# Sample-token products over 128 rows instead of 32, whole-identity transposes, and two vector transposes merged

## The chip, the core and the metric

The kernel runs on one core of a Trainium2 chip. The core has five engines with a queue each: PE (TensorE: matrix products and transposes; the profile shows its weight loads apart, as PEld), DVE (VectorE), ACT (ScalarE), POOL (GpSimd) and SP (SyncE, which here only issues DMAs). They run side by side and meet at semaphores. The metric is the time of one execution on the device in microseconds (us), as a median of several runs. Smaller is better.

## The reference: what is computed

One encoder layer for two requests at once: a prompt of 1024 tokens and 32 sample tokens that go on from a cache. Model width is 1024, everything is float32. Cut to what matters:

```python
h  = rms_norm(x, g_pre_mix);  z = h @ w_in          # q, k, v | q, f, i, og | two gates
# A: windowed attention, 16 query heads, 2 key/value heads of width 64, a sink per head
s  = q @ k.T * 64**-0.5 + bias                      # sample: 128 cached + 32 new keys
m  = max(s.max(-1), sink);  p = exp(s - m)
ya = (p / (p.sum(-1) + exp(sink - m))) @ v
# B: gated linear recurrence, 8 heads, key and value width 128, blocks of 64 (sample: 32)
o  = (q * exp(b)) @ state
a  = (q * exp(b - b_mid)) @ (k * exp(b_mid - b)).T
o  = o + where(causal, a, 0) @ v
state = exp(b_last) * state + (k * exp(b_last - b)).T @ v
yb = rms_norm(o, g_hgrn_out) * silu(og)
x  = x + rms_norm((sig(ga) * (ya @ w_br_a) + sig(gb) * (yb @ w_br_b)) @ w_out)
# conv feed-forward, then a per-layer input behind a gate
x  = x + rms_norm((gelu(conv3(a)) * u) @ w_down);  x = x + (pe @ w_ple) * sig(x @ w_ple_gate)
```

## The kernel before

Tokens lie along the free axis of most tiles, features along the 128 partitions. The 1056 tokens (1024 prompt, then 32 sample) are cut into the groups `GR` of 384, 384 and 288 columns. `token_tiles(g)` cuts a group into tiles of 128; the third tile of group 2 is the sample with its 32 tokens.

Large products run in three passes over a high and a low part of both operands (`product`, lines 200 to 202, in the first stages; lines 1006 to 1009 in the recurrence). One pass is one PE matmul with a stationary operand of 128 rows by 128 columns, which PEld loads, and 288 or 384 moving columns. A matmul of two plain float32 operands is issued as two PE instructions; a float32 transpose (a matmul against the identity `ident`) as one. In a row of the profile, "32*128 32x32" means: 32 rows contracted, 128 stationary columns, and 32 moving columns.

The stages that the change touches, in order of time:

- **Start, up to about 59 us.** Rows of `x` are loaded, normed and transposed. `turn_(g, k, b)` (line 584) transposes block k of the up to three row tiles of group g; for group 2 the third transpose has 32 rows. `h_part` (ACT line 226, DVE line 227) splits the result into `La` and `Lb`, which the products read, and `x_store` (DVE line 593) writes the scaled block away. `norm_rows` (line 301) spreads a column of factors over all partitions; its third product for group 2 has 32 rows (it is called later with tiles of 88 and 96 rows too). `vectors` (line 617) transposes four small tiles of gains and caches: 8, 41, 88 and 44 rows. `step` and `pinned` fix the order of work on the engines named; the rest is ordered by the framework's planner, from estimated times.
- **Attention, about 57 to 375 us.** A stream of products (`stream`), with the attention of one head pair i beside it. For each i from 0 to 7 and each block j from 0 to 8, `scores(i, j)` makes the probabilities in a tile `sc` (lines 451 to 467; POOL writes the sink at line 455), `turn(i, j)` transposes them (line 478) and splits them into `ph` and `pl` (ACT 223, DVE 224), and `values(i, js)` multiplies them with `Vs` (lines 500 and 501). Block j = 8 is the sample: 32 query rows, and keys in two tiles, 128 cached ones and 32 new ones (tile 9 of `Vs`).
- **Recurrence, about 375 to 870 us.** 8 heads; 22 pieces of products per head, and beside them the recurrence of the head before. `k_turn` and `v_turn` (lines 1174, 1102) transpose the decayed keys and the values of a group into `kk` and `vk`; `tile_in(h, j)` computes the state update (line 1192) and the scores (1200, for the sample 1196), masks them into `am`, and updates the state; `tile_out(h, j)` computes the output (lines 1232 and 1234); `group_out(h, g)` transposes it back (line 1255). j = 8 is the sample: 32 rows at lines 1192, 1232 and 1255, and 32 stationary columns at 1196, 1232 and 1234.

Each of these PE instructions has its operands cut to the tile's own number of rows `m_`:

```python
E.transpose(b[:, n * P:n * P + rows], t[:rows, k * P:(k + 1) * P], ident[:rows, :rows])   # turn_
E.matmul(oc, lhs, ph[:kn, a, :2 * m_], start=a == 0, stop=False)          # values, lhs = Vs[:kn, ...]
E.matmul(s[:, 256:384], kk[:m_, i, :], vk[:m_, i, :], start=True, stop=True)              # tile_in
E.matmul(b[:m_, 0:P], am[:m_, :m_], vk[:m_, i, :], start=True, stop=st is None)           # tile_out
E.transpose(t[:, c:c + m_], vk[:m_, i, :], ident[:m_, :m_])                               # group_out
```

Of the kernel before, what the change touches and what calls it, by code (L numbers as in the profile page):

```python
# [10 lines left out]
F32 = mybir.dt.float32  # L11
# [6 lines left out]
P = 128  # L18
# [41 lines left out]
def layer_kernel(  # L60
# [251 lines left out]
    with right("ap") as ap:  # L312
# [130 lines left out]
        def scores(i, j):  # L443
            m_, k0, nk, b0, tl = span(j)
            e_ = b0 + nk
            g, c = (2, SO) if j == 8 else (j // 3, (j % 3) * P)
            kv, bias = i // 4, biases[i]
            s = s_bank()
            for h, q in enumerate(qs[i, g]):
                o = s[:, h * 256 + b0:h * 256 + e_]  # L450
                E.matmul(o, q[:, c:c + P], K1[kv][:, k0:k0 + nk], start=True, stop=False)
                E.matmul(o, q[:, c:c + P], K2[kv][:, k0:k0 + nk], start=False, stop=True)
            sc = aq.tile([P, 2, 260], F32, tag="sc", name=nm("sc"), bufs=5)
            st = aq.tile([P, 2, 2], F32, tag="st", name=nm("st"), bufs=4)
# [13 lines left out]
            probs[i, j] = sc  # L468

        def turn(i, j):  # L470
            m_, k0, nk, b0, tl = span(j)
            sc = probs[i, j]
            ph = aq.tile([P, 2, 2 * P], F32R, tag="ph", name=nm("ph"), bufs=4)
            pl = aq.tile([P, 2, 2 * P], F32R, tag="pl", name=nm("pl"), bufs=4)
            t = tr_bank()
            for a, (_, kc, kn) in enumerate(tl):
                for h in range(2):
                    E.transpose(t[:kn, a * 256 + h * m_:a * 256 + (h + 1) * m_],  # L478
                                sc[:m_, h, kc:kc + kn], ident[:m_, :m_])
            if m_ == P:  # L480
                sl = [(P, slice(0, 256 * len(tl)))]
            else:
                sl = [(kn, slice(a * 256, a * 256 + 2 * m_)) for a, (_, _, kn) in enumerate(tl)]
            fh, fl = ph[:].rearrange("p a b -> p (a b)"), pl[:].rearrange("p a b -> p (a b)")
            for kn, z in sl:
                split(fh[:kn, z], fl[:kn, z], t[:kn, z])
            probs[i, j] = (ph, pl)

        def values(i, js):
# [4 lines left out]
            for x, j in enumerate(js):  # L494
                ph, pl = probs.pop((i, j))
                tl = span(j)[4]
                oc = o[:, x * 256:x * 256 + 2 * m_]
                for a, (vt_, _, kn) in enumerate(tl):
                    lhs = Vs[:kn, vt_, kv].rearrange("p a b -> p (a b)")
                    E.matmul(oc, lhs, ph[:kn, a, :2 * m_], start=a == 0, stop=False)  # L500
                    E.matmul(oc, lhs, pl[:kn, a, :2 * m_], start=False, stop=a == len(tl) - 1)
            nx = len(js)
# [36 lines left out]
        with tc.tile_pool(name="np", bufs=1, side="right", reuse_waits="tile") as np_:  # L539
            def load_tile(xt, g, n):  # L540
                t = np_.tile([P, D], F32, tag="x", name=nm("x"), bufs=8)
                xt.append((t, load_x(t, g, n, x_prompt, x_sample)))

# [37 lines left out]
            def turn_(g, k, b):  # L581
                hb[g, k] = b
                for n, (t, rows) in enumerate(xt[g]):
                    E.transpose(b[:, n * P:n * P + rows], t[:rows, k * P:(k + 1) * P],
                                ident[:rows, :rows])

# [9 lines left out]
            def vector_rows():  # L596

                g0 = np_.tile([8, P], F32, name="g0rows")
                gdma(g0[:], g_pre_mix.rearrange("o (r p) -> (o r) p", p=P))
                gv = np_.tile([41, P], F32, name="gvrows")  # L600
                for r, a, n in ((0, g_post_mix, 8), (8, g_pre_ffn, 8), (16, g_post_ffn, 8),
# [10 lines left out]
                return (g0, gvec[:, 0:8], 8), (gv, gvec[:, 8:49], 41), (cv, cvec, 88), (cr, cach, 44)  # L612

            def vectors(rows):
                for src, dst, n in rows:
                    b = tr_bank()
                    E.transpose(b[:, :n], src[:], ident[:n, :n])
                    V.tensor_copy(dst[:], b[:, :n])

            def derived():  # L620
# [357 lines left out]
    with right("bp") as bp:  # L978
# [7 lines left out]
        G.memset(resets[:], 1.0)  # L986
        G.memset(resets[:].rearrange("p (b c) -> p b c", c=64)[:, :, 0:1], 0.0)
        HD = [{} for _ in range(8)]
        ahead_b = 3
# [106 lines left out]
        def v_turn(h, g):  # L1096
            d = HD[h]
            vt = d.pop(("vt", g))
            vk = d["vk", g] = bp.tile([P, 3, P], F32, tag="vk", name=nm("vk"), bufs=4)
            t = tr_bank()  # L1100
            for i, (c, m_, smp) in enumerate(token_tiles(g)):
                E.transpose(t[:m_, i * P:(i + 1) * P], vt[:, c:c + m_], ident[:])
            f = 3 if g < 2 else 2
            S.copy(vk[:, 0:f, :], t[:, :f * P].rearrange("p (a b) -> p a b", b=P))
            if g == 2:
                S.copy(vk[:32, 2, :], t[:32, 2 * P:3 * P])

# [60 lines left out]
        def k_turn(h, g):  # L1168
# [8 lines left out]
            if g == 2:  # L1177
                S.copy(kk[:32, 2, :], t[:32, 2 * P:3 * P])
            d["kk", g] = kk

        def tile_in(h, j):
# [3 lines left out]
            c, m_, smp = token_tiles(g)[i]  # L1185
            d1, qx, kk, vk = d["d1", g], d["qx", g], d["kk", g], d["vk", g]
            if smp:
# [3 lines left out]
            s = bank(pb, "so", 2)  # L1191
            E.matmul(s[:, 256:384], kk[:m_, i, :], vk[:m_, i, :], start=True, stop=True)
            am = bp.tile([P, P], F32, tag="am", name=nm("am"), bufs=2)
            ai = am[:].bitcast(I32)
# [26 lines left out]
        def tile_out(h, j):  # L1221
# [9 lines left out]
            vk = d["vk", g]  # L1231
            E.matmul(b[:m_, 0:P], am[:m_, :m_], vk[:m_, i, :], start=True, stop=st is None)
            if st is not None:
                E.matmul(b[:m_, 0:P], d["tq", g][:, c:c + m_], st[:], start=False, stop=True)
            S.copy(vk[:m_, i, :], b[:m_, 0:P])
            sq = bp.tile([P, P], mybir.dt.bfloat16, tag="sq", name=nm("sq"), bufs=1)
            S.activation(sq[:m_], vk[:m_, i, :], AF.Square, accum_out=d["ss"][:m_, j % 6:j % 6 + 1])
            if j in (5, 8):
# [4 lines left out]
                for a in range(n):  # L1243
                    g_, i_ = (a // 3, a % 3) if j == 5 else (2, a)
                    m_ = token_tiles(g_)[i_][1]
                    os_ = d["vk", g_][:m_, i_, :]
                    S.mul(os_, os_, rs[:m_, a:a + 1])

        def group_out(h, g):
# [4 lines left out]
            for i, (c, m_, smp) in enumerate(token_tiles(g)):  # L1254
                E.transpose(t[:, c:c + m_], vk[:m_, i, :], ident[:m_, :m_])
            V.scalar_tensor_tensor(sg[:, :n], t[:, :n], ghh[:, 0:1], sg[:, :n],
# [887 lines left out]
```

## Time and profile before

| What | Value |
|---|---|
| median of 3 runs | 2002.62 us (2002.28 to 2002.85) |
| the profiled execution: its time, its span | 2002.58 us, 2000.8 us |
| granted TensorE clock | 1.000 |
| busy, share of the span: PE, PEld, DVE, ACT, POOL | 99%, 98%, 71%, 48%, 11% |
| PE matmuls, and as many weight loads | 14304 |

The span runs from the first to the last instruction of the profiled execution; 1.8 us of its time lie outside. PE's busy time goes by modelled ends of overlapping matmuls, so the start times in the order of time tell more: the distance from the start of one matmul to that of the next is what the first one costs the queue. In rows that merge several instructions ("x2"), the time is the start of the first one. PEld rows give the start of a weight load; "idle before" names what an engine waited for.

### The profile page before, as it was taken

What the parts mean: (1) busy time and instruction counts of PE and PEld (TensorE: products, weight loads), DVE (VectorE), ACT (ScalarE), POOL (GpSimd) and SP (SyncE); (2) the same over time, 40 slices, a digit from 0 to 9 for tenths busy, and PEclk for the clock granted to TensorE, in tenths of its full rate; (3) what the DMA queues carried; (4) which work ended last, traced back from release to release, by engine and by line L of the source; (5) the groups of instructions that cost most, each with busy time, mean ns of one, the idle gap of its engine ahead of it and who ended that gap; (6) DMA issues with size and microseconds to landing.
All of it is one profiled execution on the core that took longest, in us unless ns stands there. A gap on an engine that the chain in (4) does not pass through costs nothing.

```text
span 2000.8 us, 37359 instructions
## 1 busy us (share of the span) xinstructions
PE 1984.3 (99%) x14304; PEld 1955.0 (98%) x14304; DVE 1424.5 (71%) x3138; ACT 965.4 (48%) x2159; POOL 228.4 (11%) x323
## 2 busy tenths in 40 slices
PE   8999999999999999999999999999999999999998
PEld 7899999999999999999999999999999999999998
DVE  6788888688888888554455788788888784655552
ACT  7555566566666666442124663333333344444432
POOL 1110100000000000002001023333333210000000
PEclk9999999999999999999999999999999999999999
DMA  7622311411111111377558582222222245655543
GB/s 257 155 92 85 106 53 55 154 43 58 58 37 51 41 54 54 123 241 220 166 165 291 173 288 70 80 76 86 76 86 76 86 141 195 213 192 173 171 130 80
DMA packets 253639, 247.47 MB, mean 124 GB/s; under 512 B 13893, under 2 KB 221912, under 8 KB 253461
## 3 DMA queue, kind: packets, MB, share of 16 engines
q1 hardware_dynamic: 245141, 218.59, 35.3%
q0 software_dynamic: 8240, 26.44, 3.7%
q8 instruction: 112, 1.84, 0.4%
q14 instruction: 66, 0.54, 0.1%
q10 hardware_dynamic: 80, 0.07, 0.0%
HBM read 177.56 MB, written 65.32 MB: 121 GB/s over the span
## 4 chain that ended last, share of the span: by engine, by line
PE 92%; DVE 4%; ACT 2%; DMA 1%; issue 1%; POOL 0%; SPq 0%; DVEq 0%; ACTq 0%; POOLq 0%
PE mm L200 14%; PE mm L201 14%; PE mm L202 14%; PE st L1867 7%; PE st L1866 7%; PE st L1865 7%; PE G L1009 2%; PE Y L1006 2%; PE G L1008 2%; PE G L1006 2%; PE Y L1009 2%; PE Y L1008 2%; PE tr L478 1%; PE X L1006 1%; PE so L1200 1%; PE X L1009 1%
## 5 line engine op out<-in xcount | busy, mean ns | idle before, releaser
L1865 PE MATMUL st<-op,wt 128*128 128x264 f32 x1232 | 348.6, 283 | 2.0 <-DVE Sp L1878 1.3
L1867 PE MATMUL st<-op,wt 128*128 128x264 f32 x1232 | 349.8, 284 | 0.0
L1866 PE MATMUL st<-op,wt 128*128 128x264 f32 x1232 | 347.6, 282 | 0.0
L184 DVE TENSOR_TENSOR wl<-wr,wh 128x1024 fp32r<-128x1024 f32 x129 | 157.9, 1224 | 120.7 <-ACT wh L181 111.7
L1865 PEld LDWEIGHTS st<-op,wt 128*128 128x128 f32 x1232 | 231.2, 188 | 3.5 <-DVE Sp L1878 1.7
L1866 PEld LDWEIGHTS st<-op,wt 128*128 128x128 f32 x1232 | 231.4, 188 | 0.0
L1867 PEld LDWEIGHTS st<-op,wt 128*128 128x128 f32 x1232 | 230.9, 187 | 0.0
L181 ACT CAST wh<-wr 128x1024 fp32r<-128x1024 f32 x116 | 121.8, 1050 | 197.7 <-PE mm L201 136.1
L200 PE MATMUL mm<-La,wh 128*128 128x384 f32 (+1 forms) x528 | 174.4, 331 | 0.0
L201 PE MATMUL mm<-Lb,wh 128*128 128x384 f32 (+1 forms) x528 | 170.9, 324 | 0.6 <-DVE Lb L710 0.6
L200 PE MATMUL mm<-ac,wh 128*128 128x352 f32 x528 | 170.8, 323 | 0.0
L202 PE MATMUL mm<-La,wl 128*128 128x384 f32 (+1 forms) x528 | 170.5, 323 | 0.2 <-DVE wl L685 0.2
L202 PE MATMUL mm<-ac,wl 128*128 128x352 f32 x528 | 169.8, 322 | 0.0
L201 PE MATMUL mm<-ac,wh 128*128 128x352 f32 x528 | 169.3, 321 | 0.0
L1625 ACT CAST wt<-wu 128x512 fp32r<-128x512 f32 x126 | 77.9, 619 | 186.6 <-POOL ab L1851 88.3
L200 PE MATMUL mm<-Ra,wh 128*128 128x264 f32 x512 | 145.4, 284 | 0.0
L201 PE MATMUL mm<-Rb,wh 128*128 128x264 f32 x512 | 145.0, 283 | 0.0
L202 PE MATMUL mm<-Ra,wl 128*128 128x264 f32 x512 | 145.0, 283 | 0.0
L1626 DVE TENSOR_TENSOR wt<-wu,wt 128x512 fp32r<-128x512 f32 x126 | 103.0, 820 | 39.0 <-ACT wt L1625 39.0
L462 ACT ACTIVATE sc<-sc,st 128x257 f32<-128x257 f32 (+1 forms) x144 | 69.7, 485 | 74.0 <-DVE st L457 73.0
L201 PEld LDWEIGHTS mm<-Lb,wh 128*128 128x128 f32 x528 | 99.4, 188 | 1.7 <-DVE Lb L710 1.4
L202 PEld LDWEIGHTS mm<-La,wl 128*128 128x128 f32 x528 | 99.2, 188 | 0.7 <-DVE wl L685 0.5
(496 smaller groups left out, 5694.8 us busy)
## 6 DMA issues: line engine op xcount, KB each, us to landing
wr<-in_w_down_dram SPq DMA_DIRECT2D x66, 512.0 KB
wu<-in_w_up_dram SPq DMA_DIRECT2D x42, 512.0 KB
wu<-in_w_in_dram SPq DMA_DIRECT2D x32, 512.0 KB
wr<-in_w_in_dram SPq DMA_DIRECT2D x25, 512.0 KB
ac<-act_d SPq DMA_DIRECT2D x66, 176.0 KB
act_d<-Up SPq DMA_DIRECT2D x21, 528.0 KB
wr<-in_w_out_dram SPq DMA_DIRECT2D x16, 512.0 KB
pw_d<-pw POOLq DMA_DIRECT2D x11, 512.0 KB, 5.6
```

The costliest lines, as they stand in the source:

```text
L181: S.copy(hi[:], raw[:])
L184: V.tensor_tensor(lo[:], raw[:], hi[:].bitcast(F32), op=ALU.subtract)
L200: E.matmul(ps, wh, a, start=first and n == 0, stop=False)
L201: E.matmul(ps, wh, b, start=False, stop=False)
L202: E.matmul(ps, wl, a, start=False, stop=last and n == len(ks) - 1)
L1006: E.matmul(o, wh, x[0][k], start=first and k == 0, stop=False, skip_group_check=True)
L1008: E.matmul(o, wh, x[1][k], start=False, stop=False, skip_group_check=True)
L1009: E.matmul(o, wl, x[0][k], start=False, stop=k == 3, skip_group_check=True)
L1626: V.tensor_tensor(t[:, 1], src, t[:, 0].bitcast(F32), op=ALU.subtract)
L1865: E.matmul(o, wh, xh, start=first and k == 0, stop=False, skip_group_check=True)
L1866: E.matmul(o, wh, xl, start=False, stop=False, skip_group_check=True)
L1867: E.matmul(o, wl, xh, start=False, stop=k == 3, skip_group_check=True)
```

## The change

Every product and transpose of the sample's 32 tokens that contracted 32 rows now contracts 128, with zeros in the rows beyond 32 of one operand at least. Transposes use the whole `ident`, and so have 128 moving columns where they had 32.

- `turn_`: whole tiles; POOL clears rows 32 to 127 of the sample's row tile in `load_tile`, with two memsets.
- `norm_rows`: all its products contract as many rows as the largest tile has (the factors of unused rows are finite, and `ident[:r, :m_]` has zeros there).
- `vectors`: the cached rows (44) share a tile with the gains (41), so that one transpose of 85 rows takes the place of two; the two copies out of PSUM stay.
- attention, j = 8: the probabilities lie in one tile of its own, `sc8`, cleared once by POOL; the four transposes are 128 by 128, the result is split by one ACT and one DVE instruction over four blocks of 32 columns where there were two of each, and `values` contracts 128 rows; tile 9 of `Vs` is cleared once.
- recurrence, j = 8: the sample's values and outputs lie in one tile `vk_s`, its masked scores in `am_s`, both cleared once; the sample's rows of `kk` beyond 32 are cleared by two POOL memsets per head. `vk` has three buffers for groups 0 and 1, and `vk2` one for group 2.

```diff
     def norm_rows(rs, tiles, out):
-        n = sum(m_ for _, m_ in tiles)
+        n, r = sum(m_ for _, m_ in tiles), max(m_ for _, m_ in tiles)
...
-            E.matmul(t[:, c:c + m_], rs[:m_, i:i + 1].to_broadcast([m_, P]), ident[:m_, :m_],
+            E.matmul(t[:, c:c + m_], rs[:r, i:i + 1].to_broadcast([r, P]), ident[:r, :m_],
...
-            sc = aq.tile([P, 2, 260], F32, tag="sc", name=nm("sc"), bufs=5)
+            sc = sc8 if j == 8 else aq.tile([P, 2, 260], F32, tag="sc", name=nm("sc"), bufs=5)
...
-                    E.transpose(t[:kn, a * 256 + h * m_:a * 256 + (h + 1) * m_],
-                                sc[:m_, h, kc:kc + kn], ident[:m_, :m_])
+                    E.transpose(t[:, (2 * a + h) * P:(2 * a + h + 1) * P], sc[:, h, kc:kc + P],
+                                ident[:])
...
-                    lhs = Vs[:kn, vt_, kv].rearrange("p a b -> p (a b)")
-                    E.matmul(oc, lhs, ph[:kn, a, :2 * m_], start=a == 0, stop=False)
+                    lhs = Vs[:, vt_, kv].rearrange("p a b -> p (a b)")
+                    E.matmul(oc, lhs, ph[:, z], start=a == 0, stop=False)
...
+                if rows < P:
+                    G.memset(t[32:64], 0.0)
+                    G.memset(t[64:P], 0.0)
...
-                    E.transpose(b[:, n * P:n * P + rows], t[:rows, k * P:(k + 1) * P],
-                                ident[:rows, :rows])
+                    E.transpose(b[:, n * P:(n + 1) * P], t[:, k * P:(k + 1) * P], ident[:])
...
-                cr = np_.tile([44, P], F32, name="crows")
-                gdma(cr[:], cache_ffn_conv[0, 0].rearrange("j (r p) -> (j r) p", p=P))
+                gdma(gv[41:85], cache_ffn_conv[0, 0].rearrange("j (r p) -> (j r) p", p=P))
...
+                G.memset(Vs[:, 9].bitcast(F32), 0.0)
...
+        sc8 = aq.tile([P, 2, 2 * P], F32, name="sc8")
+        G.memset(sc8[:], 0.0)
...
+                G.memset(kk[32:64, 2, :], 0.0)
+                G.memset(kk[64:P, 2, :], 0.0)
...
+            kk, vk = d["kk", g][:, i, :], vk_s if smp else d["vk", g][:, i, :]
...
-            E.matmul(s[:, 256:384], kk[:m_, i, :], vk[:m_, i, :], start=True, stop=True)
+            E.matmul(s[:, 256:384], kk, vk[:], start=True, stop=True)
...
-            E.matmul(b[:m_, 0:P], am[:m_, :m_], vk[:m_, i, :], start=True, stop=st is None)
+            E.matmul(b[:m_, 0:P], am[:, :m_], vk[:], start=True, stop=st is None)
...
-                E.transpose(t[:, c:c + m_], vk[:m_, i, :], ident[:m_, :m_])
+                E.transpose(t[:, c:c + P], vk_s[:] if smp else vk[:, i, :], ident[:])
```

More of the change, by code (lines that the diff above doesn't have):

```diff
@@ L497, in values @@
                 oc = o[:, x * 256:x * 256 + 2 * m_]
-                for a, (vt_, _, kn) in enumerate(tl):
-                    lhs = Vs[:kn, vt_, kv].rearrange("p a b -> p (a b)")
-                    E.matmul(oc, lhs, ph[:kn, a, :2 * m_], start=a == 0, stop=False)
-                    E.matmul(oc, lhs, pl[:kn, a, :2 * m_], start=False, stop=a == len(tl) - 1)
+                for a, (vt_, _, _) in enumerate(tl):
+                    lhs = Vs[:, vt_, kv].rearrange("p a b -> p (a b)")
+                    z = slice(2 * a * m_, 2 * (a + 1) * m_)
+                    E.matmul(oc, lhs, ph[:, z], start=a == 0, stop=False)
+                    E.matmul(oc, lhs, pl[:, z], start=False, stop=a == len(tl) - 1)
             nx = len(js)
@@ L541, in load_tile @@
                 t = np_.tile([P, D], F32, tag="x", name=nm("x"), bufs=8)
[L542 removed]
+                rows = load_x(t, g, n, x_prompt, x_sample)
+                xt.append((t, rows))
+                if rows < P:
+                    G.memset(t[32:64], 0.0)
+                    G.memset(t[64:P], 0.0)
             def sums_tile(g):
@@ L987, in layer_kernel @@
         G.memset(resets[:].rearrange("p (b c) -> p b c", c=64)[:, :, 0:1], 0.0)
+        vk_s, am_s = (bp.tile([P, n], F32, name=nm("z")) for n in (P, 32))
+        for t in (vk_s, am_s):
+            G.memset(t[:], 0.0)
         HD = [{} for _ in range(8)]
@@ L1098, in v_turn @@
             vt = d.pop(("vt", g))
-            vk = d["vk", g] = bp.tile([P, 3, P], F32, tag="vk", name=nm("vk"), bufs=4)
+            tag, f, bufs = ("vk", 3, 3) if g < 2 else ("vk2", 2, 1)
+            vk = d["vk", g] = bp.tile([P, f, P], F32, tag=tag, name=nm("vk"), bufs=bufs)
             t = tr_bank()
@@ L1102, in v_turn @@
                 E.transpose(t[:m_, i * P:(i + 1) * P], vt[:, c:c + m_], ident[:])
-            f = 3 if g < 2 else 2
             S.copy(vk[:, 0:f, :], t[:, :f * P].rearrange("p (a b) -> p a b", b=P))
             if g == 2:
-                S.copy(vk[:32, 2, :], t[:32, 2 * P:3 * P])
+                S.copy(vk_s[:32], t[:32, 2 * P:3 * P])
         def decay(h):
@@ L1191, in tile_in @@
             s = bank(pb, "so", 2)
-            E.matmul(s[:, 256:384], kk[:m_, i, :], vk[:m_, i, :], start=True, stop=True)
-            am = bp.tile([P, P], F32, tag="am", name=nm("am"), bufs=2)
+            E.matmul(s[:, 256:384], kk, vk[:], start=True, stop=True)
+            am = am_s if smp else bp.tile([P, P], F32, tag="am", name=nm("am"), bufs=2)
             ai = am[:].bitcast(I32)
@@ L1244, in tile_out @@
                     g_, i_ = (a // 3, a % 3) if j == 5 else (2, a)
-                    m_ = token_tiles(g_)[i_][1]
-                    os_ = d["vk", g_][:m_, i_, :]
+                    _, m_, smp = token_tiles(g_)[i_]
+                    os_ = vk_s[:m_] if smp else d["vk", g_][:, i_, :]
                     S.mul(os_, os_, rs[:m_, a:a + 1])
```

31 lines of the change are left out of this document (17 added, 14 removed).

## The prediction

> **What bounds the kernel now.** I read the page first: the share of each engine, then the chain that ended last.
>
> ```profile
> PE 1984.3 (99%) x14304; PEld 1955.0 (98%) x14304; DVE 1424.5 (71%) x3138; ACT 965.4 (48%) x2159; POOL 228.4 (11%) x323
> ...
> PE 92%; DVE 4%; ACT 2%; DMA 1%; issue 1%; POOL 0%; SPq 0%; DVEq 0%; ACTq 0%; POOLq 0%
> ```
>
> PE is busy for 99% of the span and makes up 92% of the chain. Shares are averages, so next come the two stages that hold most of the change, attention and recurrence (length, then busy time of PE, PEld, DVE, ACT, POOL, the granted clock, the DMA share and GB/s):
>
> ```profile
> 57.00:375.00 318.00, 315.72 (x2178) 308.36 (x2178) 253.53 (x805) 183.21 (x555) 33.72 (x129) 1.00 0.28 86
> 418.00:870.00 452.00, 451.49 (x2971) 438.84 (x2970) 362.51 (x1024) 275.58 (x744) 0.00 (x0) 1.00 0.22 66
> ```
>
> PE stands still for 2.3 us in the first and 0.5 us in the second, at full clock; DVE, the next engine, is busy for 80% of each (253.53 / 318, 362.51 / 452). So what shortens PE's queue there should shorten the run, until DVE comes near. A PE row's duration is a latency that the next instruction overlaps, so all prices below are distances between starts, from the order of time on PE. The yardsticks of undisturbed work with 128 rows:
>
> ```profile
> 437.92 0.49 PE L1102 MATMUL tr<-ident,vt 128*128 128x128 f32 x3
> 438.25 0.39 PE L1192 MATMUL so<-vk,kk 128*128 128x128 f32 x2
> 438.47 0.49 PE L1200 MATMUL so<-qx,d 128*128 128x192 f32 x2
> ```
>
> Three transposes take 0.33 us (438.25 - 437.92), two float32 matmul instructions 0.22: 0.11 us for each instruction.
>
> **The change part by part.** Each place in the order of time, what it takes now, and what it takes by the yardsticks.
>
> *Attention, transposes of the sample (line 478), once for each of 8 head pairs.* With the weight loads (PEld) of the products before:
>
> ```profile
> 186.62 0.33 PE L201 MATMUL mm<-Lb,wh 128*128 128x384 f32 x1
> 186.62 0.19 PEld L202 LDWEIGHTS mm<-La,wl 128*128 128x128 f32 x1
> 186.79 0.34 PE L202 MATMUL mm<-La,wl 128*128 128x384 f32 x1
> 187.06 0.36 PE L478 MATMUL tr<-ident,sc 32*128 32x32 f32 x4
> 187.35 0.44 PE L200 MATMUL mm<-La,wh 128*128 128x384 f32 x1
> 187.63 0.33 PE L201 MATMUL mm<-Lb,wh 128*128 128x384 f32 x1
> ```
>
> A product of 384 columns takes 0.17 (186.79 - 186.62). Before the transposes it takes 0.27 and after them 0.28: a gap of 0.10 where rows go from 128 to 32, one of 0.11 on the way back, although the four small transposes themselves need only 0.29. In all 0.84 (187.63 - 186.79); after, 2 x 0.17 + 4 x 0.11 = 0.78. Saved: 0.06. The wider transposes eat most of what the gaps give.
>
> Here one rule speaks against the change. The row first: the load of line 202 starts at 186.62, together with the matmul of line 201 before it, though both use all 128 rows; it is done ahead. The Trainium skill (TensorE: Matmul & The Clock Gate, Part 3: Packing small matmuls) has it that a weight load overlaps running matmuls only where the row groups differ. By that, work padded to 128 rows could not load ahead; the trace of this kernel disagrees, so the sum goes by 0.11, and what the rule would make of it is a rival below.
>
> *Attention, values (lines 500, 501), 8 times:*
>
> ```profile
> 193.07 0.19 PE L500 MATMUL o<-ph,Vs 128*128 128x64 f32 x1
> 193.10 0.28 PE L501 MATMUL o<-pl,Vs 128*128 128x64 f32 x1
> 193.30 0.29 PE L500 MATMUL o<-ph,Vs 32*128 32x64 f32 x1
> 193.44 0.27 PE L501 MATMUL o<-pl,Vs 32*128 32x64 f32 x1
> 193.64 0.44 PE L478 MATMUL tr<-ident,sc 128*128 128x128 f32 x2
> 194.05 0.29 PE L201 MATMUL mm<-Lb,wh 128*128 128x288 f32 x1
> ```
>
> From 193.07 to 194.05 lie four value products, two transposes and a product of 288 columns: 0.98. No chain of four products of 64 columns on 128 rows exists in the trace; its cost per instruction lies between 0.03 (193.07 to 193.10, with the load long done) and 0.11 (twice the columns, the same load). I take 0.11, because the load of 128 columns stays. After: 6 x 0.11 + 0.13 (the 288 product, quoted below) = 0.79. Saved: 0.19; at the low price 0.5.
>
> *Recurrence, state update and scores of the sample (lines 1192, 1196), 8 times:*
>
> ```profile
> 467.09 0.39 PE L1234 MATMUL so<-S,tq 128*128 128x128 f32 x2
> 467.40 0.48 PE L1192 MATMUL so<-vk,kk 32*128 32x128 f32 x2
> 467.82 0.25 PE L1196 MATMUL so<-qx,d 128*32 128x32 f32 x2
> 468.00 0.55 PE L1174 MATMUL tr<-ident,ke 128*128 128x128 f32 x3
> ```
>
> Line 1234 takes 0.31 instead of 0.22 and line 1192 takes 0.42 instead of 0.22, 0.91 to the start of the transposes. Line 1196 keeps its 32 columns, so from 1192 to it the shape still changes, in columns alone. Whether that costs, the next place shows.
>
> *Recurrence, output of the sample (lines 1232, 1234), 8 times:*
>
> ```profile
> 471.90 0.34 PE L1009 MATMUL Y<-TH,wt 128*128 128x384 f32 x1
> 472.17 0.40 PE L1232 MATMUL so<-vk,am 32*32 32x128 f32 x2
> 472.50 0.41 PE L1234 MATMUL so<-S,tq 128*32 128x128 f32 x2
> 472.84 0.55 PE L1255 MATMUL tr<-ident,vk 128*128 128x128 f32 x3
> ```
>
> From line 1234 to 1255 only the columns change (32 to 128), and two instructions take 0.34, so a change of columns costs about 0.10 too. Line 1232 becomes 128 rows by 32 columns, the form of 1234: the gap between those two goes (0.33 to 0.24), the one behind shrinks by 0.02, since 1234 no longer loads late; the gaps at both ends stay. Saved: 0.11. In the place before, I keep 0.10 between 1192 and 1196: 0.22 + 0.22 + 0.10 + 0.18 = 0.72, saved 0.19. If changes of columns cost nothing once the rows stay at 128, another 0.10 and 0.22 go.
>
> *Recurrence, transposes of the sample's output (line 1255), 8 times:*
>
> ```profile
> 483.32 0.56 PE L1255 MATMUL tr<-ident,vk 128*128 128x128 f32 x3
> 483.81 0.45 PE L1006 MATMUL X<-La,wt 128*128 128x384 f32 x1
> 484.10 0.34 PE L1008 MATMUL X<-Lb,wt 128*128 128x384 f32 x1
> ```
>
> 0.78 for three transposes (the third with 32 rows) and a product; after, 0.33 + 0.17 = 0.50. Saved: 0.28.
>
> Per head: 0.06 + 0.19 + 0.19 + 0.11 + 0.28 = 0.83; times 8, **6.6 us**.
>
> *Start.* `turn_` of group 2, 8 times:
>
> ```profile
> 50.45 0.30 PE L200 MATMUL mm<-La,wh 128*128 128x288 f32 x1
> 50.58 0.55 PE L584 MATMUL s<-ident,x 128*128 128x128 f32 x3
> 51.07 0.40 PE L201 MATMUL mm<-Lb,wh 128*128 128x288 f32 x1
> 51.30 0.29 PE L202 MATMUL mm<-La,wl 128*128 128x288 f32 x1
> ```
>
> A product of 288 columns takes 0.13 (50.58 - 50.45). Transposes and one product: 0.72 now, 0.33 + 0.13 = 0.46 after; 0.26 saved, 2.1 for 8. `norm_rows` of group 2 and the transposes of 41 and 44 rows are the same exchange, 0.26 each as an estimate from these rows, and the merged one is gone with its 0.11: 0.9 more, 3.0 in all. Not all of it need arrive, for here other engines run close behind (waits from 40 to 62 us):
>
> ```profile
> DVE Lb L227 <- ACT La L226: 5.0, 6, 2.2
> ACT La L226 <- PE s L584: 1.7, 3, 0.7
> ACT La L226 <- PE o L584: 0.8, 1, 0.8
> ```
>
> ACT waits 2.5 us for just these transposes and DVE waits for ACT, so they can follow by about that much, less what their own queues then need. Ends 0 and 3.0; I take **2.0 us**.
>
> *Added work off the path.* POOL gets some 22 memsets. Its row for a memset and its longest wait in the start:
>
> ```profile
> 73.15 0.20 POOL L430 MEMSET bias<- 64x128 f32 x1 [8.38 <-DMA bias<-rb_d]
> POOL K L338 <- ACT kh L223: 47.1, 1, 47.1
> ```
>
> At 0.20 per 128 columns, the two of 1024 columns take at most 1.6 us each, inside the 47 us in which POOL waits; `sc8` (512 columns, 0.8) is wanted only when j = 8 comes. The sixteen on `kk` fall where POOL does nothing (0.00 in the row of the recurrence), eight pieces ahead of their reader. Uncovered, they would cost 8 x 0.4 = 3.2. ACT and DVE lose one instruction each per sample turn; that is off the path and counted at nothing, as are the buffers: `vk2`, `vk_s`, `am_s` and `sc8` are read out well before the next head writes them.
>
> *Sum.* 6.6 + 2.0 = 8.6 us, from the profiled 2002.58 (span 2000.8, so 1.8 outside) to 1994.0. The median, 2002.62, is the same to 0.04.
>
> **The rivals.**
>
> 1. *The start's gain goes into waits.* DVE's own queue holds the attention back, and PE waits for it later. Then 6.6: 1996.0. For it: attention begins only with the bias at 73.15. Against: that wait is at the end of a chain which PE's own transposes start. 0.10.
> 2. *Changes of columns cost nothing* with rows at 128: (0.10 + 0.22) x 8 = 2.6 more, 1991.4. For: the 32-column transposes cost nothing extra. Against: 0.34 from 1234 to 1255. 0.08.
> 3. *The gaps hang on something else than rows* (waits, operands), so the change doesn't do what it says. They stay, and the four transposes at line 478 grow from 0.29 to 0.44: 8 x 0.15 = 1.2, less 0.4 for the dropped one, 2003.4. Against: gaps at every change of form. 0.06.
> 4. *Loads are no longer ahead.* The eleven padded instructions of a head cost 0.19 each, the load's duration, instead of 0.11: 88 x 0.08 = 7.0, and 2001.0. The row at 186.62 is against it. 0.02. (It is the rule named above.)
> 5. *Slower: attention becomes bound by DVE and ACT.* PE reaches each turn earlier, DVE and ACT have hardly less to do, and the planner may order the queues anew, so that turns come before their probabilities. One such wait exists:
>
> ```profile
> PE tr L478 <- DVE pl L224: 0.7, 1, 0.7
> ```
>
> With 72 turns, it decides from about 12 late ones on (12 x 0.7 = 8.4). A third late: 24 x 0.7 = 16.8, less 8.6, 2010.8. Against: only one among 72 so far, DVE 80% busy. 0.06.
>
> **How the numbers follow.** The forecast, 1994.0, has 0.68 and its own range 1992 to 1996. Below, rival 2 with the whole start (6.6 + 2.6 + 3.0 = 12.2) gives 1990.4; above, the start lost and two more waits of about 1 us give 1998. That is the range. What a measurement of this kernel can tell from no change is 0.2%, 4.0 us, so faster means under 1998.6: forecast and rivals 1 and 2, 0.86. Same: rivals 3 and 4, 0.08. Slower: rival 5, 0.06.
>
> **What would show it.** No PE row with 32 rows but that of line 650; the place at 187 takes 0.78, that of line 1255 takes 0.50, the values 0.79; line 1192 keeps a gap behind it, before 1196, and 1232 one ahead of it. The recurrence shortens by 8 x 0.58 = 4.6 us with PE as full as now, the attention by 2.0. It would be wrong if 0.20 or more still stands before the padded instructions, if PE's idle time between 57 and 375 us grows by what it saved, or if products wait for POOL.

## The result, and the profile after

The changed kernel takes 1995.1 us (median of 6 runs, 1993.13 to 1996.65), the kernel before 2002.73 (6 runs, 2001.82 to 2003.68): a ratio of 0.9961, with a 95% interval of 0.9948 to 0.9974, or 7.6 us. The forecast was 1994.0 with a range of 1990.4 to 1998.0. On a second chip the same kernel took 1994.28 against 2000.47, 0.9967 (0.9955 to 0.998). The profiled execution took 1993.55, its span is 1991.8.

The page of the changed kernel: engines, then the chain that ended last.

```profile
PE 1974.8 (99%) x14303; PEld 1954.3 (98%) x14303; DVE 1422.5 (71%) x3130; ACT 962.7 (48%) x2151; POOL 235.4 (12%) x345
...
PE 91%; DVE 4%; ACT 1%; issue 1%; DMA 1%; POOL 0%; SPq 0%; DVEq 0%; POOLq 0%; ACTq 0%
```

PE still bounds the kernel. It executes one instruction fewer and is 9.5 us less busy (1984.3 before): its instructions stand closer together. POOL has exactly 22 instructions more (345 against 323). The two large stages again, in the columns of the prediction:

```profile
57.00:375.00 318.00, 315.97 (x2196) 312.55 (x2196) 256.39 (x801) 183.86 (x552) 35.31 (x132) 1.00 0.29 89
418.00:870.00 452.00, 450.96 (x3012) 442.59 (x3011) 363.36 (x1029) 278.90 (x751) 3.31 (x17) 1.00 0.24 72
```

More PE instructions fit into the same stretches (2196 against 2178, 3012 against 2971). PE's idle time in the first is 2.03 us (318 - 315.97; 2.75 in a second profile of the same kernel, 2.28 before), in the second 1.04 (0.54 in the second profile, 0.51 before).

Now the places of the prediction, in the changed kernel's order of time on PE. First the transposes and the values of the attention:

```profile
183.77 0.34 PE L202 MATMUL mm<-La,wl 128*128 128x384 f32 x1
183.94 0.60 PE L478 MATMUL tr<-ident,sc 128*128 128x128 f32 x4
184.29 0.43 PE L200 MATMUL mm<-La,wh 128*128 128x384 f32 x1
184.56 0.33 PE L201 MATMUL mm<-Lb,wh 128*128 128x384 f32 x1
...
189.97 0.19 PE L501 MATMUL o<-ph,Vs 128*128 128x64 f32 x1
190.00 0.28 PE L502 MATMUL o<-pl,Vs 128*128 128x64 f32 x1
190.11 0.28 PE L501 MATMUL o<-ph,Vs 128*128 128x64 f32 x1
...
190.75 0.29 PE L201 MATMUL mm<-Lb,wh 128*128 128x288 f32 x1
```

The product ahead of the transposes now takes 0.17 (183.94 - 183.77) where it took 0.27: the gap is gone. The product behind them still takes 0.27 (184.56 - 184.29; 0.28 before), and the four transposes take 0.35 (184.29 - 183.94). So the 0.11 that the prediction read as a gap on the way back is not one: a product behind transposes of 128 rows takes as long. The whole place takes 0.79 (184.56 - 183.77; 0.84 before, 0.78 forecast); that sum doesn't depend on how it is shared out between the transposes and the product. The values take 0.78 (190.75 - 189.97; 0.98 before, 0.79 forecast). The value products follow each other after 0.11, as taken. Then the three places of the recurrence:

```profile
462.65 0.39 PE L1249 MATMUL so<-S,tq 128*128 128x128 f32 x2
462.87 0.39 PE L1207 MATMUL so<-z,kk 128*128 128x128 f32 x2
463.19 0.25 PE L1211 MATMUL so<-qx,d 128*32 128x32 f32 x2
463.37 0.55 PE L1186 MATMUL tr<-ident,ke 128*128 128x128 f32 x3
...
467.26 0.34 PE L1021 MATMUL Y<-TH,wt 128*128 128x384 f32 x1
467.53 0.41 PE L1247 MATMUL so<-z,z 128*32 128x128 f32 x2
...
468.09 0.55 PE L1270 MATMUL tr<-ident,vk 128*128 128x128 f32 x3
...
478.57 0.38 PE L1270 MATMUL tr<-ident,vk 128*128 128x128 f32 x2
...
479.08 0.33 PE L1020 MATMUL X<-Lb,wt 128*128 128x384 f32 x1
```

State update and scores take 0.72 (463.37 - 462.65; 0.91 before, 0.72 forecast), the output 0.56 (468.09 - 467.53; 0.67 before, 0.11 less as forecast), its transposes and the product behind them 0.51 (479.08 - 478.57; 0.78 before, 0.50 forecast). The gaps that were to remain are there too: 0.32 from line 1207 to 1211, and 0.27 from the product of line 1021 to line 1247, where 32 stationary columns come or go. In the whole trace only the two instructions of line 657 still contract 32 rows.

One row of each trace sums the recurrence up. It groups the sample's scores (two instructions for each of 8 heads): smallest, median and largest duration in ns, first and last start in us. Before:

```profile
L1196 PE MATMUL so<-qx,d x16: 196/206/217, 467.8 to 844.1; 128*32 128x32 f32 x16
```

After:

```profile
L1211 PE MATMUL so<-qx,d x16: 196/206/217, 463.2 to 835.6; 128*32 128x32 f32 x16
```

From the first head to the last lie 376.3 us before and 372.4 after. In all but the last step, one head follows the other by 54.74 us before and 54.11 to 54.13 after: 0.62 less, 0.58 forecast.

Where the time came from, by the moment at which the first instruction of a stage starts on PE (us; the kernels of the experiments are described below):

| | bias rows L650/L657 | cached rows L391 | recurrence L1006/L1018 | products behind it | last transpose |
|---|---|---|---|---|---|
| before | 58.21 | 88.62 | 385.79 | 871.56 | 1996.31 |
| after | 56.06 | 86.79 | 381.37 | 862.80 | 1986.87 |
| after, again | 55.65 | 87.42 | 382.03 | 862.97 | 1987.60 |
| start alone | 57.03 | 88.19 | 384.60 | 869.89 | 1993.40 |
| attention alone | 58.11 | 88.02 | 383.36 | 868.27 | 1992.27 |
| recurrence alone | 57.81 | 88.04 | 385.22 | 867.02 | 1991.96 |
| 32 rows again | 57.48 | 87.51 | 384.57 | 869.85 | 1993.85 |

After against before: 4.4 us are won up to the recurrence and 4.3 in it (485.77 to 481.43). From there to the end lie 1124.75 and 1124.07; the change does nothing there, and other profiles of kernels that share that part vary as much (1123.51 start alone, 1124.94 recurrence alone). Single profiles scatter in the recurrence too. The one of before is the longest of the four without the recurrence's part of the change: 485.77, against 485.29 (start alone), 484.91 (attention alone) and 485.28 (32 rows again), 485.3 on the mean. Against that mean the changed kernel wins 3.9 us there, and 4.4 in its second profile.

### The profile page after: what moved, and what is told of

Read it like the earlier page. It is cut to its first block, busy times and chain, and to the rows that moved or that the text cites. A ratio compares the mean times of both kernels' runs of the same rounds, so it can differ in the third digit from the quotient of the medians.

```text
span 1991.8 us, 37378 instructions
## 1 busy us (share of the span) xinstructions
PE 1974.8 (99%) x14303; PEld 1954.3 (98%) x14303; DVE 1422.5 (71%) x3130; ACT 962.7 (48%) x2151; POOL 235.4 (12%) x345
## 4 chain that ended last, share of the span: by engine, by line
PE 91%; DVE 4%; ACT 1%; issue 1%; DMA 1%; POOL 0%; SPq 0%; DVEq 0%; POOLq 0%; ACTq 0%
PE mm L200 14%; PE mm L201 14%; PE mm L202 14%; PE st L1882 7%; PE st L1881 7%; PE st L1880 7%; PE Y L1018 2%; PE G L1021 2%; PE G L1020 2%; PE G L1018 2%; PE Y L1021 2%; PE Y L1020 2%; PE tr L478 1%; PE so L1215 1%; PE Z L1021 1%
```

## The experiments

Theory: PE loses about 0.10 us each time its instructions go from 128 contracted rows to 32 or back, and the change takes those times away. Rivals: the buffers, the merged instructions or the new order of the queues brought the gain; the start's share goes into waits; the last changes of form, in columns, cost nothing.

**The parts, each alone.** Each kernel is the kernel before with one part of the change. At the start:

```diff
-                    E.transpose(b[:, n * P:n * P + rows], t[:rows, k * P:(k + 1) * P],
-                                ident[:rows, :rows])
+                    E.transpose(b[:, n * P:(n + 1) * P], t[:, k * P:(k + 1) * P], ident[:])
```

with `norm_rows`, `vectors` and the memsets of `load_tile`.

> Only the edits of the start (row transposes of the sample, norm rows, merged vector transposes); attention and recurrence as before. Theory (PE pays for each change of the rows contracted): the start's first product with the relative-bias table comes 2.1 us earlier, as in the changed kernel, PE keeps 1.8 of it, and the time falls by about 1.8 us, too little to tell from no change by the timed runs alone, but the recurrence takes as long as before, with 54.74 us per head. Rival (the start's gain is lost later): time as before within 0.5 us and PE's waits between 57 and 95 us larger by 2.

In the attention:

```diff
-                    E.matmul(oc, lhs, ph[:kn, a, :2 * m_], start=a == 0, stop=False)
+                    E.matmul(oc, lhs, ph[:, z], start=a == 0, stop=False)
```

with the transposes of line 478, `sc8` and tile 9 of `Vs`.

> Only the edits of the attention (own tile for the sample's probabilities, whole transposes, values over 128 rows). Theory: 8 x 0.27 us less PE queue between 87 and 367 us, so about 2.2 us less in all; one sample turn with its neighbours takes 0.78 us instead of 0.84, one values step 0.77 instead of 0.98. Rival (ACT and DVE instructions saved, or another order, make the gain): the two steps keep their length and the gain lies elsewhere, or the time falls by less than 1.

In the recurrence:

```diff
-            E.matmul(s[:, 256:384], kk[:m_, i, :], vk[:m_, i, :], start=True, stop=True)
+            E.matmul(s[:, 256:384], kk, vk[:], start=True, stop=True)
```

with the sample's outputs and their transposes, `vk_s`, `am_s` and the memsets on `kk`.

> Only the edits of the recurrence (own tiles for the sample's values and masked scores, cleared rows, 128 rows at the state update, output and output transposes). Theory: a head takes 54.13 us instead of 54.74 on PE, 8 x 0.6 = 4.9 us less, minus up to 0.5 that the last head gave back as a wait in the changed kernel: time lower by 4.4 to 4.9 us. Rival (POOL's sixteen memsets cost something, in DVE's or PE's waits): less than 4.

Measured, against 2001.31 for the kernel before on that chip (33 runs): start 2000.53, 0.9997 (0.9988 to 1.0006); attention 2000.27, 0.9994 (0.9985 to 1.0002); recurrence 1997.4, 0.998 (0.9971 to 0.9989). Only the recurrence is told from no change by its time. The traces tell more. In the attention alone the recurrence begins at 383.36; in the two kernels with neither start nor attention edits it begins at 385.79 and 385.22, 385.5 on the mean: 2.1 us from the attention, 2.0 forecast. In the recurrence alone the heads follow after 54.11 to 54.13 us, just as in the whole change; in the two others after 54.73. The recurrence shortens by 4.0 us there (481.80 against 485.77; 3.5 against the mean of 485.3), 4.6 forecast. The start alone begins the recurrence 0.9 us earlier.

Against what was expected of each: for the start, 1.8 us less, and 0.8 came, which its interval tells neither from nothing nor from 1.8; the first product with the bias table came 1.2 us earlier, not 2.1. For the attention, 2.2 us, and 1.0 came, with an interval that still holds 2.2; its two steps have the lengths expected (0.79 and 0.77). For the recurrence, 4.4 to 4.9, and 3.9 came (2.2 to 5.8 by its interval), just on the side of the rival, which had POOL's memsets cost something and less than 4 us won. But the heads follow each other as the theory has it, and no PE instruction of that recurrence waits for POOL; most of what is missing stands in the last head, as shown further below.

**The rows taken back.** The changed kernel with its buffers, its memsets, its merged transpose of 85 rows and its schedule made anew, but with the operands cut to 32 rows again, and the sample's probabilities split by two ACT and two DVE instructions as before:

```diff
-            E.matmul(s[:, 256:384], kk, vk[:], start=True, stop=True)
+            E.matmul(s[:, 256:384], kk[:m_], vk[:m_], start=True, stop=True)
...
-                    E.transpose(b[:, n * P:(n + 1) * P], t[:, k * P:(k + 1) * P], ident[:])
+                    E.transpose(b[:, n * P:n * P + rows], t[:rows, k * P:(k + 1) * P],
+                                ident[:rows, :rows])
```

> The changed kernel with all its tiles, buffers, memsets and the merged vector transposes, but PE's operands cut to the sample's rows again (32 rows, and two splits per sample turn as before). Theory: the gaps come back at every place, time 2002 to 2003 us, that of before less about 0.4 for the merged transposes. Rival (buffers, tiles or the planner's order made the gain): time near the changed kernel's, 1995 to 1998.

2001.25 us, 1.0001 (0.9993 to 1.001): the gain is gone. (The 2002 to 2003 that were expected came from the first chip's 2002.73; the kernel before takes 2001.31 on this one.) The gaps are back in its order of time on PE:

```profile
465.85 0.39 PE L1252 MATMUL so<-S,tq 128*128 128x128 f32 x2
466.16 0.48 PE L1210 MATMUL so<-z,kk 32*128 32x128 f32 x2
...
466.75 0.55 PE L1189 MATMUL tr<-ident,ke 128*128 128x128 f32 x3
```

465.85 to 466.75 is 0.90 (0.91 before, 0.72 after), and a head takes 54.71 to 54.73 us. So it is the rows; what else the change rearranged is worth nothing that these times can tell. In its trace, though, the recurrence begins at 384.57, as early as with the start alone (384.60). So the 0.9 us above can't be put down to the start's padded rows: the merged transpose, which this kernel keeps, or the scatter of single profiles may account for it.

**The forms by themselves.** A kernel with nothing but PE instructions, in an order written out: three instructions of one form between runs of eight products of 384 columns (float32r, 128 rows, 0.174 us from one to the next). It computes none of the reference's results.

```diff
+            for _ in range(3):
+                pin(f)
+            for _ in range(8):
+                pin(product)
```

> Computes none of the layer: only a chain of products of 384 columns with 128 rows and 128 stationary columns, into which three instructions (six for float32 matmuls) of another form are set, each form twice. Theory: no gap for 128 or 96 rows or columns, about 0.10 us before and about 0.10 after for 32 rows, and for 32 columns in matmuls but not in transposes; 64 rows or columns as 32; inside a run of one form nothing. Rival (the gap belongs to the change of weights or operands, not to the form): the same gap for all forms, or for none.

Its order of time on PE; the form is stationary rows * columns, then the moving operand (x6 are three float32 matmuls of two instructions each):

```profile
17.12 0.83 PE L42 MATMUL form<-x 128*128 128x128 f32 x6
17.71 1.66 PE L39 MATMUL base<-xr 128*128 128x384 f32 x8
19.21 0.83 PE L42 MATMUL form<-x 96*128 96x128 f32 x6
19.79 1.67 PE L39 MATMUL base<-xr 128*128 128x384 f32 x8
21.39 0.93 PE L42 MATMUL form<-x 64*128 64x128 f32 x6
22.25 1.68 PE L39 MATMUL base<-xr 128*128 128x384 f32 x8
...
29.25 1.66 PE L39 MATMUL base<-xr 128*128 128x384 f32 x8
30.84 0.87 PE L42 MATMUL form<-x 128*64 128x128 f32 x6
31.64 1.68 PE L39 MATMUL base<-xr 128*128 128x384 f32 x8
...
50.15 1.66 PE L39 MATMUL base<-xr 128*128 128x384 f32 x8
51.64 0.49 PE L48 MATMUL form<-ident,x 128*32 128x128 f32 x3
51.89 1.64 PE L39 MATMUL base<-xr 128*128 128x384 f32 x8
```

Read the distances. Eight products take 1.50 ahead of 96 rows (19.21 - 17.71) and 1.60 ahead of 64 (21.39 - 19.79): the 0.10 gap. It is 1.61 and 1.60 ahead of 32 and 16. The six instructions take 0.59 with 128 rows, 0.58 with 96, and 0.86 with 64, 32 or 16 alike. So going to a smaller form and back costs 0.37 in all, for each of 64, 32 and 16 rows, and nothing for 96. Every form stands twice in the run, and the second time agrees within 0.02. Fewer columns cost 1.59 and 0.80 (64 columns), nearly as much. But transposes with 32 stationary columns cost nothing: 1.49 ahead of them, 0.25 for three, 0.24 with 128 columns. Neither do float32r matmuls with 64 or 32 columns (1.52 and 1.47 ahead), while float32r with 64 or 32 rows pays the gap like the others (1.57 and 1.59 ahead; three take 0.45, against 0.25 with 128 rows). So do transposes of 32 rows: 1.60 ahead, and 0.29 for three, although they move 32 columns and not 128.

The weight loads show what happens at a gap. The first load of 96 rows, and the first of 64:

```profile
19.03 0.82 PEld L42 LDWEIGHTS form<-x 96*128 96x128 f32 x6
...
21.39 0.74 PEld L42 LDWEIGHTS form<-x 64*128 64x128 f32 x6 [0.25 <-issue]
```

With 96 rows the load starts at 19.03, 0.18 ahead of its own matmul (19.21), while the product before still runs. With 64 rows it starts at 21.39, together with its own matmul, after PEld has stood idle for 0.25. So at a gap the load is not done ahead; why, the trace does not say.

The Trainium skill (TensorEngine Tiling (Array Packing), Available Configurations and Key Properties) lists 128, 64 and 32 rows, and likewise columns, as tiling modes, and says that a change of mode drains TensorE; it gives no price. The probe agrees for rows: 96 cost as little as 128, and 64, 32 and 16 pay. For columns it agrees only in plain float32 matmuls.

**The columns as well.** What remained in the changed kernel, 128*32 forms, given 128 stationary columns, with the unused ones cleared or ignored (this takes two more memsets per head, and the values of groups 0 and 1 get two buffers instead of three):

```diff
-                E.matmul(s[:32, 0:32], d1[:, c:c + 32], qx[:, 384:416]
+                E.matmul(s[:, 0:32], d1[:, c:c + P], qx[:, 384:416]
...
-            E.matmul(b[:m_, 0:P], am[:, :m_], vk[:], start
+            E.matmul(b[:, 0:P], am[:], vk[:], start
...
-                E.matmul(b[:m_, 0:P], d["tq", g][:, c:c + m_], st[:]
+                E.matmul(b[:, 0:P], d["tq", g][:, c:c + P], st[:]
```

Beside it the changed kernel once more, on the same chip.

> The changed kernel once more, beside the next one on the same chip. 1993 to 1997 us by its first six runs, 5.5 to 9 less than before; the profile again 54.13 us per head.

> The changed kernel, and in the recurrence the sample's masked scores and output also use 128 stationary columns instead of 32 (the columns beyond 32 cleared by two more POOL memsets per head; two buffers instead of three for the values of groups 0 and 1). Theory (PE pays the same for a change of columns as of rows): the step of state update and scores loses its two changes, 0.21 + 0.05 + 0.13 + 0.05 to about 0.11 + 0.11 + 0.11, and the output step 0.27 + 0.13 + 0.11 + 0.11 + 0.20 + 0.05 to 0.17 + 4 x 0.11; about 0.37 us per head, 54.13 to 53.76, 3.0 us in all. Rival (columns alone cost nothing, what is seen there is the late load after a change of rows): the gaps stay at 0.20 or the time does not fall.

The changed kernel: 1994.28 (5 runs), and the wide one 1991.85 (5 runs), 0.9953 (0.9939 to 0.9966) against the kernel before. On another chip:

> The kernel with 128 stationary columns for the sample once more, on the same chip as the two above, as their yardstick and to see whether its ratio of 0.9953 to the kernel before holds: 0.994 to 0.9966, and 53.73 us per head in the recurrence again.

1992.07, 0.995 (0.9936 to 0.9963). Its order of time on PE:

```profile
463.36 0.39 PE L1253 MATMUL so<-S,tq 128*128 128x128 f32 x2
463.58 0.39 PE L1211 MATMUL so<-z,kk 128*128 128x128 f32 x2
463.80 0.31 PE L1215 MATMUL so<-qx,d 128*128 128x32 f32 x2
463.95 0.52 PE L1190 MATMUL tr<-ident,ke 128*128 128x128 f32 x3
```

Line 1211 now takes 0.22 (0.32 in the changed kernel), the place 0.59 (0.72). A head takes 53.71 to 53.73 us, 0.39 to 0.40 less (0.37 expected), so the last changes of form did cost something. This is the best of the versions tried: about 2.4 us less than the changed kernel on the chip that ran both (their intervals overlap), and 8.6 and 9.5 us less than the kernel before on the two chips.

**Where the start's gain goes.** In the start the prices were right too, as the turns of group 2 show in the changed kernel:

```profile
49.99 0.49 PE L589 MATMUL s<-ident,x 128*128 128x128 f32 x3
...
50.46 0.29 PE L201 MATMUL mm<-Lb,wh 128*128 128x288 f32 x1
```

0.47 for three transposes and a product (0.72 before, 0.46 forecast). But less arrives at the recurrence. From 44 to 100 us PE is busy for (first number after the comma) 54.46 us before:

```profile
44.00:100.00 56.00, 54.46 (x351) 49.45 (x352) 40.66 (x125) 33.90 (x91) 9.88 (x27) 1.00 0.58 149
```

and 53.84 in the kernel with the start's part alone:

```profile
44.00:100.00 56.00, 53.84 (x359) 50.37 (x360) 41.69 (x126) 34.15 (x93) 10.38 (x28) 1.00 0.60 156
```

Idle time there, for the kernels with the start's part: 2.16 (alone), 1.38 and 1.94 (the changed kernel twice), 2.89 and 1.71 (the wide one twice), 2.0 on the mean; for those without it 1.54 (before), 0.97 and 1.30 (attention and recurrence alone), 1.3. So on the mean some 0.75 of the gain turns into waits, but the kernels with the start's part differ among themselves by twice that (1.38 to 2.89), so the size is not firm.

A candidate for what holds PE back was SP's queue: in the changed kernel the bias rows are ready at 57.46 us but their store is issued at 58.56 only, behind issues of K. To test it, one line moves the store to ACT's queue:

```diff
-                dma(rb_d[:], nrb[:].unsqueeze(1).to_broadcast([16, 24, 384]))
+                S.dma_start(rb_d[:], nrb[:].unsqueeze(1).to_broadcast([16, 24, 384]))
```

> The changed kernel, with one edit: the bias rows are stored by ACT's queue instead of SP's. In the changed kernel the rows are ready at 57.46 us (L658) and SP issues their store only at 58.56, behind three issues of K at 56.72 to 58.47; in the kernel before the rows were ready at 59.61 and the store left at 59.64. Theory A, the start's gain is held up in SP's queue: the store leaves within 0.2 us of the end of L658, the first bias memset (71.64 after, 73.15 before) comes about 1 us earlier against L657 than in the changed kernel (15.6 us behind L657 there, 14.6 here), and the run is 0.5 to 1.0 us shorter, near 1994. Rival B, it is held up behind that, by SP's later issues or by ACT's wait for the next weights (L181 <- DMA wr, 1.03 us in the changed kernel): the store leaves earlier, the memset or the first transposes of cached rows do not, and the time is within 0.3 us of the changed kernel's. Rival C: ACT pays for the issue (some 0.6 us ahead of its table load at 58.24), and the run is longer.

> The same edit on the kernel with 128 stationary columns for the sample (wide_cols, 1991.85). Theory A: 0.5 to 1.0 us less, 1990.9 to 1991.4. Rival B: within 0.3 us of wide_cols. Rival C: longer.

Theory A and rival B both missed the time. Rival C had it longer, and it is, but not for C's reason: ACT's issue takes 0.67 us (58.49 to 59.16). The changed kernel with this line takes 2002.84, 1.0005 (0.9996 to 1.0014), the wide one 2000.18, 0.9993 (0.9984 to 1.0002): 8 us lost, by the move of one store (the wide one takes 1992.07 on this chip without it). The store does leave at once (rows ready at 58.45, issue at 58.49). But the planner orders the start anew. SP's issues in that kernel:

```profile
58.24 7.51 SPq L338 DMA_DIRECT2D K<-kh  x4
65.84 3.03 SPq L338 DMA_DIRECT2D K<-kl  x4
69.06 2.82 SPq L429 DMA_DIRECT2D bias<-rb_d  x4
```

Eight issues of K now stand ahead of the bias loads (six in the changed kernel), which leave at 69.06 instead of 67.25. The bias is ready 15.9 us after line 657 (15.6 in the changed kernel), no sooner. And PE's order now has products behind scores (line 451) that wait for DVE's line 457, which needs the bias:

```profile
66.21 0.34 PE L202 MATMUL mm<-La,wl 128*128 128x384 f32 x1
73.91 0.58 PE L451 MATMUL s<-K,qa 128*128 128x256 f32 x1 [7.36 <-DVE st L457]
...
74.93 0.52 PE L200 MATMUL mm<-La,wh 128*128 128x384 f32 x1
75.25 0.52 PE L201 MATMUL mm<-Lb,wh 128*128 128x384 f32 x1
```

PE stands for 7.36 us, and then runs more slowly: 0.32 from one product of 384 columns to the next instead of 0.17. The windows show the granted clock (the first number after the busy times) at 0.91 from 68 to 70, at 0.50 from there to 78, and at 0.53 from 78 to 80, so at half until about 79.9. One of them:

```profile
76.00:78.00 2.00, 2.00 (x9) 1.90 (x8) 1.28 (x6) 0.83 (x1) 0.32 (x2) 0.50 0.90 226
```

The Trainium skill (TensorE: Matmul & The Clock Gate, Part 1) has it that PE falls to half its clock after an idle window of about 3.4 us; the 0.50 behind this wait of 7.36 us agrees. Rival B holds in so far as SP's later issues, not the store, set the time of the bias. Which single wait takes the 0.75 us in the changed kernel itself was not isolated: the profiles with the start's part show short waits for ACT (line 391, 0.2 to 0.8), for DVE (line 378, 0.2 to 0.6) and, in some, ahead of line 451 (0.2 to 0.4).

## Why the prediction was right

*The gaps.* Right in size at every place, and right in the cause; one reading was wrong, the 0.11 behind the transposes of line 478, which is there with 128 rows too (0.27). What the way back costs lies inside the time of the small instructions themselves, as the probe shows (0.86 for six instead of 0.59). Of the five places with a gap, all are within 0.01 us of the forecast, and the kernel with its rows cut again has lost the whole gain. Rival 3 (something else than rows) falls by that. Rival 4 (loads no longer ahead) falls by the value products, 0.11 apart with loads of 0.19; so does the rule of the Trainium skill behind it (TensorE: Matmul & The Clock Gate, Part 3: Packing small matmuls), as far as this kernel shows it.

*Columns.* Kept at 0.10 between lines 1207 and 1211 and ahead of 1247, and that is what stands there. Rival 2 falls. Its other half, that 32-column transposes cost nothing, was a true observation with a narrower reach: the probe shows that it holds for transposes and float32r, not for plain float32 matmuls.

*Attention.* 2.0 forecast, 2.1 measured, by one profile against two that differ by 0.6 themselves. PE did not run ahead of DVE and ACT: between 57 and 375 us it is idle for 2.03 and 2.75 us in the two profiles, 2.28 before. Rival 5, the slower one, falls.

*Recurrence.* 4.6 forecast. Against the mean of the four profiles without this part, 485.3, it is 3.9 in the profile after, 4.4 in its second profile and 3.5 with the recurrence alone (against the one of before alone, 4.3, 4.8 and 4.0). Eight heads at 0.62 would give 5.0. Most of the difference lies in the last head, which the prediction did not price. PE there, after:

```profile
813.38 0.49 PE L1247 MATMUL so<-vk,am 128*128 128x128 f32 x2 [1.04 <-DVE S L1225]
```

and before:

```profile
821.61 0.49 PE L1232 MATMUL so<-vk,am 128*128 128x128 f32 x2 [0.51 <-DVE S L1210]
```

The wait is 1.04 against 0.51 here, 0.54 in the second profile of the changed kernel and 1.42 with the recurrence alone; with the start alone, the attention alone and the 32 rows again PE does not wait there at all. What PE waits for, the state that DVE writes at 813.03, stands in DVE's queue behind a split of weights (line 184), that one behind ACT's cast of them, and the cast behind their load. ACT in the changed kernel:

```profile
810.21 1.05 ACT L181 CAST wh<-wr 128x1024 fp32r<-128x1024 f32 x1 [3.49 <-DMA wr<-in_w_in_dram]
```

and DVE:

```profile
811.29 1.23 DVE L184 TENSOR_TENSOR wl<-wr,wh 128x1024 fp32r<-128x1024 f32 x1 [6.24 <-ACT wh L181]
```

The same cast stands at 818.45 before. It came forward by 8.2 us, PE's work ahead of the wait by 8.8 (820.62 to 811.85), and the wait grew by the 0.5 between.

*Start.* The term that was mis-sized most. 2.0 was taken between 0 and 3.0, on the reading that DVE and ACT follow by what they had waited for the transposes. They do follow: the bias rows start 2.2 and 2.6 us earlier in the two profiles of the changed kernel, 1.2 in the start alone. But part of it is lost behind them. From line 657 (650 before) until the bias has come and POOL can write it (line 430) it is 14.7 to 15.0 us in the three profiles without any of the start's edits, and 15.1 to 15.6 in the five with its padded rows. The four profiles that hold both the start's and the attention's parts (the changed kernel and the wide one, twice each) begin the recurrence at 381.37, 382.03, 383.23 and 382.06, 382.2 on the mean; with the attention alone it is 383.36. So about 1.2 us arrive and not 2.0, though the four differ by 1.9 among themselves and the attention alone is one profile. With the start alone it is 0.9, which the kernel with 32 rows again has as well. Rival 1 holds by somewhat less than half.

*The sum.* 1.2 + 2.1 + 3.9 (the mean of the three recurrences, against 485.3) = 7.2, where 8.6 was forecast; the medians differ by 7.6, and by 6.2 on the second chip. The start is short by 0.8 and the recurrence by 0.7; the attention gave 0.1 more.

*Work at nothing.* POOL's 22 memsets add 7.0 us of busy time (235.4 - 228.4), and no PE instruction waits for POOL between 57 and 375 us or in the recurrence. They are hidden, as forecast; the two of 1024 columns take 0.95 us each, where the prediction allowed 1.6.

## What to carry to other kernels

On a queue of PE that is full, look at the distances between starts where the form changes: instructions with 64, 32 or 16 contracted rows among instructions with 128 cost about 0.10 us on the way in and more until the next product starts (0.27 for six float32 instructions here), so zeros that fill the rows are cheaper than few rows, as long as the padded instructions stream no more than the gap is worth. The same holds for stationary columns of plain float32 matmuls, not for transposes or float32r. Price such a gain in full only where PE is the one that is late; where other engines and transfers run close behind, as in the start here, perhaps half of it arrives; and do not move a transfer to another queue without looking at what a planner then puts in front of the waiting engine.

## What was not expected of the hardware

- 64 rows cost as much as 32 or 16 (0.86 for six instructions each, 0.59 with 128), and 96 cost nothing (0.58).
- Columns count only in plain float32 matmuls: eight products take 1.59 ahead of 64 such columns, but 1.52 ahead of 64 and 1.47 ahead of 32 in float32r, and 1.49 ahead of a transpose of 32.
- At a gap the weight load is not done while the product before it runs: it starts at 21.39 for a matmul at 21.39 with 64 rows, but at 19.03 for one at 19.21 with 96.
- After a wait of 7.36 us PE's granted clock stayed at 0.50 for some 6 us of work (73.9 to about 79.9), so that a wait costs more than its length. The kernel with the moved store is 8 us longer.
